# A down projection by seven products with the tokens moving, the last gate as modulation sections, the residual in device memory

## The chip, the cores and the metric

The kernel runs on one core of a Trainium2 chip. The metric is device time in microseconds (us) of one execution; the figure given for a kernel is the median of its runs. TensorE (PE) multiplies, VectorE (DVE), ScalarE (ACT) and GpSimd (POOL) work elementwise, and SyncE (SP) issues nearly all transfers between device memory and the on-chip memory.

## The reference

One layer of a diffusion backbone is applied to 128 context tokens and 512 latent tokens, all in float32, D_MODEL = 1024, D_FF = 2816. The context tokens are modulated by `c_ctx`, the latent ones by `c`; the weights are shared.

```python
mod = (silu(cond) @ w_ada + b_ada)[:, None, :]
sh1, sc1, g1, sh2, sc2, g2 = split(mod, 6, axis=-1)
h = rms(x, norm_mix) * (1 + sc1) + sh1
mix, k, v = mixer(h, ...)              # attention and a gated short convolution, output projection
x = x + g1 * mix
h2 = rms(x, norm_ffn) * (1 + sc2) + sh2
gate, up = split(h2 @ w_gate_up, 2, axis=-1)
x = x + g2 * ((silu(gate) * up) @ w_down)
```

The last gate `g2` is one section of the modulation: 1024 numbers for the context, 1024 for the latent tokens. The outputs are x of both kinds of tokens, and the context's k and v.

## The kernel before

All 640 tokens (`TOK`) are worked on together, as five tiles of 128 (`TORD`: the context first, then four latent tiles); `HALF` is 320 of them. Every float32 product is made as three products of rounded halves: `split` (lines 151 and 152) makes a high part on ScalarE and the rest on VectorE, and `mm3` (lines 155 to 157) multiplies high by high, high by low and low by high into one PSUM bank.

**The stages**, in us from the start of the span: until 50 the first modulation sections, normalisation and h; until 251 the projections of q, k, v, the attention, and between its steps the convolution and the modulation sections (2) to (4); until 314 the output projection with the residual `x2`, the second normalisation and the transposes into `h2` (`h2_turn`, line 1012); then the feed-forward until the end.

**Modulation sections** are made by `ada_all`: for each half section of 512 columns four loads (`aw`, 512 KB each, `AWB` = 2 buffers) and eight matmuls of a padded copy of the conditioning vectors (`cond_mm`, line 394) into one bank, then four small transposes that sum the bank's strips (line 446), then an evict that adds the bias. It is a generator: it is a part of the `filler`, and at every `F1` in the order `SEQ` one step of the filler is emitted between steps of the attention.

**The last gate** is made in another way. `g2_step` (lines 1032 to 1043) multiplies rows of w_ada by one conditioning number per partition and accumulates, on VectorE, 128 x 512 at a time; `g2_out` (lines 1045 to 1052) sums over the partitions by a matmul with ones (line 1051), which leaves the gate on all partitions, and adds the bias. The first half is done during the output projection, the second during the first down projection.

**The feed-forward** takes w_gate_up in 22 blocks of 128 rows, f = 0 to 21. The first two (`NPLAIN`) are plain products. Each of the others is one product of 2 x 2 blocks (gate and up by the two halves of D on the weights' side, the two halves of D by the two halves of the tokens on the other) made by seven products in place of eight (Winograd's form): `ff_a` to `ff_end`, lines 1214 to 1257. The weights' operands are the blocks A11, A12, A22, A21 and the sums S1 to S4, made by `op_load` (lines 194 to 217: sums on VectorE at line 206, then `split`); the activations' operands B and T are made once from `h2` (`b_plain`, `b_sums`). Each product is four k-steps of three matmuls of 128 x 320: the weights are stationary, the 320 tokens move. Where two sums share a partial sum, ScalarE copies the bank into a second one (line 1241 for instance) and TensorE adds to both.

**The down projection** comes after each of four groups of blocks (`GCUT` = 0, 6, 12, 17, 22), in `down` (lines 1256 to 1294). Here the split activations `gT` are stationary, 128 tokens each, and rows of w_down move, 512 columns (in the last group's last tile 256):

```python
mm3(ps[:, :n], gT[f][0][:, s], gT[f][1][:, s], wh[:, i, c0:c0 + n], wl[:, i, c0:c0 + n],
    f == grp[0], f == grp[-1])
```

For each of two column halves and five token tiles one bank is summed over the group, multiplied by the gate (line 1291, `dm`), and added to `x2` (line 1292). In the last group the sum is stored from there. So `x2`, the residual, stays on chip from the output projection to the end.

**What sets the order.** On TensorE the order is written out by hand all through. On the other engines it is by hand until the second plain block is done, and after that a scheduler places each instruction by priority (`early(n)` moves one forward). All loads are issued by SP in one planned order (`plan`, then `W` takes them), a fixed number ahead of their use, into rings: `wf` of three buffers for raw weights, `wh` and `wl` of four for operands. PSUM in the feed-forward is six banks for products ("f") and two for transposes.

Of the kernel before, what the change touches and what calls it, by code (L numbers as in the profile page):

```python
# [9 lines left out]
F32 = mybir.dt.float32  # L10
# [28 lines left out]
SEQ = ('c0 k1 q4 k4 C0 k0 K4 Q4 a0 q0 F1 k2 K0 a1 t0 k3 t1 K1 o0 F1 Q0 o1 K2 K3 q1 F1 S0.0 F1 F1 F1 S0.1 F1 '  # L39
# [10 lines left out]
GCUT = [0, 6, 12, 17, 22]  # L50
# [25 lines left out]
AWB = 2  # L76
# [7 lines left out]
PLACE = 48, 72  # L84
# [7 lines left out]
def build(ctx, tc, x_prompt, x_sample, c, cache_k, cache_v, c_ctx, norm_mix, norm_ffn, w_ada, b_ada,  # L92
# [76 lines left out]
    open_pool("F", "right", "placeF of y oz ysum m0 g1 rs5 cp")  # L169
# [24 lines left out]
    def op_load(e):  # L194
# [3 lines left out]
        a11, a12, a21, a22 = g[:, 0:4], g[:, 4:8], u[:, 0:4], u[:, 4:8]  # L198
        if name[0] == "S":
            if name == "S12":  # L200
                sums[f] = T("sx", (P, 8, P), F32, 2)
            s13, s24 = sums[f][:, 0:4], sums[f][:, 4:8]
            with early(SOP[f >= NPLAIN]):
                for out, x, y, op in {"S12": ((s13, a21, a22, ALU.add), (s24, s13, a11, ALU.subtract)),
                                      "S34": ((s13, a11, a21, ALU.subtract), (s24, a12, s24, ALU.subtract))}[name]:
                    dve.tensor_tensor(out, x, y, op)  # L206
            src = sums[f]
        else:
            src = {"A1": g, "A2": u, "A22": a22}[name]
        if name == "A22":  # L210
            w = T(("wh", "wl")[ops[0] % 2], (P, 2, 4, P), F32R, WHB)
            ops[0] += 1
            e[5] = w[:, 0], w[:, 1]
        else:
            e[5] = T("wh", (P, 8, P), F32R, WHB), T("wl", (P, 8, P), F32R, WHB)
        with early(SOP[f >= NPLAIN]):
# [54 lines left out]
    ADA = [(2, 0), (2, 1), (3, 0), (3, 1), (4, 0), (4, 1)]  # L271
# [6 lines left out]
    for n, (off, ct) in enumerate(CONV + [(None, 0)]):  # L278
        if off is not None:
            plan(("conv", off, ct), wi[:, :, off + ct * P:off + (ct + 1) * P])  # L280
        for sec, j, h in ada_steps[2 * n - 2:2 * n if off is not None else None] if n else ():
            col = sec * D + j * 512
            plan(("ada", sec, j, h), wa[:, 2 * h:2 * h + 2, col:col + 512], 1, "a")
    for j in range(2):
        for kp in range(4):
            plan(("o", j, kp), wo[:, 2 * kp:2 * kp + 2, j * 512:(j + 1) * 512], 2 * j, "w", V_AON + 2 * kp)
        for kp in range(0 if j else 4):
            plan(("ada", 5, j, kp), wa[:, 2 * kp:2 * kp + 2, 5 * D + j * 512:5 * D + (j + 1) * 512], 2, "f")

    GROUPS = [list(range(a, b)) for a, b in zip(GCUT, GCUT[1:])]  # L290
    PLAIN, PRODS = ("A1", "A2"), ("A1", "S12", "A22", "S34")
    PAIRS = {"A11": ("A1", 0), "A12": ("A1", 4), "A21": ("A2", 0), "A22": ("A2", 4),
             "S1": ("S12", 0), "S2": ("S12", 4), "S3": ("S34", 0), "S4": ("S34", 4)}

    def plan_raw(f, x, ph=3):
        col = f * P + (DFF if x == "u" else 0)
        plan((x, f), wg[:, :, col:col + P], ph, "f")
# [5 lines left out]
    G2KP = {0: (0,), 1: (1,), 2: (2, 3)}  # L303
    for gi, grp in enumerate(GROUPS):
        for f in grp:
            ph = 2 if f < NPLAIN else 3
            plan_raw(f, "g", ph)
            plan_raw(f, "u", ph)
            plan_ops(f, PLAIN if f < NPLAIN else PRODS, ph)
        for j in range(2):  # L310
            for i0 in range(0, len(grp), 2):
                n = len(grp[i0:i0 + 2])
                plan(("d", grp[i0], j), wd[:, grp[i0]:grp[i0] + n, j * 512:(j + 1) * 512], 2)
                if gi == 0 and j == 0:
                    for kp in G2KP[i0 // 2]:
                        plan(("ada", 5, 1, kp), wa[:, 2 * kp:2 * kp + 2, 5 * D + 512:6 * D], 2, "f")
# [414 lines left out]
    def conv_steps(ct):  # L731
# [22 lines left out]
        for i, _ in enumerate(conv_mm(O_GB, ct, bps)):  # L754
# [4 lines left out]
            yield  # L759
        ysq = ysum if ct == 0 else T("c25", (P, PADW), F32, 3)[:, :PADW - 2]  # L760
# [6 lines left out]
    def ada_all():  # L767
        for sec, j in ADA:
            rp = PB(tag="c")
            for h in range(4):  # L770
# [3 lines left out]
                if h == 1:  # L774
                    yield
# [11 lines left out]
            else:  # L787
                ps = mod_sum(res, 4, "c")
                if sec == 4:
                    mod_evict(1, 4 * j, 4, ps, None)  # L790
                else:
                    mod_evict(1, 4 * j, 4, None, ps)

    ada_gen = ada_all()
# [17 lines left out]
    filler = itertools.chain(*(conv_steps(ct) for ct in range(4)), ada_some(12))  # L812
    NFILL = 12 * 6 + 12
# [178 lines left out]
    open_pool("X", "left", "x2 x2n g2 sx")  # L992
    open_pool("GT", "left", "gT")
    open_pool("Y1", "left", "B11 B21")
    open_pool("D", "right", "mix mx aacc bb")
# [6 lines left out]
    x2n = {}  # L1002
    TORD = [CTX] + list(range(NL))
# [24 lines left out]

    g2 = [T("g2", (P, D), F32, 2) for _ in range(2)]
    g2acc = [None, None]  # L1030

    def g2_step(j, kp):

        w = W(("ada", 5, j, kp))
        for i in range(2):
            k = 2 * kp + i
            for cc in range(2):
              with early(G2P) if G2P and j == 0 else ExitStack():
                if k == 0:
                    g2acc[cc] = T("cg", (P, TOK), F32, 2)[:, :512] if j else T("aacc", (P, 512), F32, 2)  # L1040
                    dve.tensor_scalar_mul(g2acc[cc], w[:, i], cs[:, k, cc:cc + 1])
                else:
                    dve.scalar_tensor_tensor(g2acc[cc], w[:, i], cs[:, k, cc:cc + 1], g2acc[cc], ALU.mult, ALU.add)

    def g2_out(j):
        cols = slice(j * 512, (j + 1) * 512)
        bb = T("cu", (P, TOK), F32, 2)[:, :512] if j else T("bb", (P, 512))
        sp.dma_start(bb, b_ada[0, 5 * D + j * 512:5 * D + (j + 1) * 512].partition_broadcast(P))
        for cc in range(2):
            ps = PB()  # L1050
            pe.matmul(ps, ones, g2acc[cc], start=True, stop=True)
            dve.tensor_tensor(g2[cc][:, cols], ps, bb, ALU.add)


# [25 lines left out]
    def b_sums(part):  # L1080
# [4 lines left out]
        def diff(x, y, z):  # L1085
            w[x] = T("tr", (P, 4, 192), F32, 3)[:, :, :n]
# [11 lines left out]
    for j in range(2):  # L1098
        cols = slice(j * 512, (j + 1) * 512)
        for n, t in enumerate(TORD):  # L1100
# [26 lines left out]
            if j == 0 and G2N <= n < 4 + G2N:  # L1127
                g2_step(0, n - G2N)
            if j == 1 and n == 0:
                g2_out(0)  # L1130
# [251 lines left out]
```

## Time and profile before

| | us |
|---|---|
| median of 3 runs | 747.73 |
| lowest and highest of them | 747.54, 748.13 |
| the profiled execution's own time | 747.58 |
| its span | 745.8 |
| TensorE busy | 729.5 (98%) |
| VectorE busy | 529.8 (71%) |
| ScalarE busy | 375.6 (50%) |
| GpSimd busy | 48.6 (7%) |

The times of instructions come from one profiled execution, whose span starts with the first and ends with the last thing recorded; its own time is 1.8 us longer. TensorE's matmuls overlap in the record, since a product's start does not wait for the end of the one before it: what a product takes from the time is the distance between two starts, not its duration. The granted clock is full in all slices.

### The profile page before, as it was taken

How to read it: one execution, taken by the hardware profiler on the slowest of the kernel's cores; microseconds unless marked ns; L12 is line 12 of the kernel's file. 1: busy time of each engine (PE TensorE's matmuls, PEld its weight loads, DVE VectorE, ACT ScalarE, POOL GpSimd, SP SyncE). 2: the span in 40 equal slices, each digit the busy share in tenths (PEclk: the TensorE clock that was granted, in tenths of full speed). 3: DMA queues.
4: the chain of work that ended last, by engine and by line, in shares of the span. 5: the costliest groups of instructions: out<-in, count | busy, mean ns of one | idle time of the engine just before them, and what ended most of it. 6: DMA issues, size and time to landing. Idle time of an engine off the chain costs nothing.

```text
span 745.8 us, 11640 instructions
## 1 busy us (share of the span) xinstructions
PE 729.5 (98%) x4556; PEld 657.5 (88%) x4556; DVE 529.8 (71%) x905; ACT 375.6 (50%) x701; POOL 48.6 (7%) x85
## 2 busy tenths in 40 slices
PE   7999899999999999999999999999999999999997
PEld 5568878988998887899998799998899998899986
DVE  5668878685666797888869767864668765677653
ACT  5357877676766544765552135552135541354510
POOL 2403201002010210000000000000000000000000
PEclk9999999999999999999999999999999999999999
DMA  9985133523424363032336314224014132123312
GB/s 288 294 248 165 43 113 104 167 93 117 152 92 147 109 225 114 26 89 57 114 97 195 89 31 112 76 95 142 28 57 113 57 113 86 57 75 96 105 65 85
DMA packets 101387, 84.50 MB, mean 113 GB/s; under 512 B 3502, under 2 KB 81650, under 8 KB 101332
## 3 DMA queue, kind: packets, MB, share of 16 engines
q1 hardware_dynamic: 100980, 83.39, 36.6%
q8 instruction: 36, 0.59, 0.4%
q0 software_dynamic: 352, 0.37, 0.3%
q14 instruction: 19, 0.16, 0.1%
HBM read 79.68 MB, written 2.75 MB: 111 GB/s over the span
## 4 chain that ended last, share of the span: by engine, by line
PE 85%; DVE 6%; DMA 3%; ACT 3%; issue 2%; POOL 1%; SPq 0%; ACTq 0%; DVEq 0%; POOLq 0%
PE pf L155 19%; PE pf L156 19%; PE pf L157 19%; PE pc L723 3%; PE pc L725 3%; PE pc L724 3%; PE pt L862 3%; PE po L879 2%; PE ps L835 2%; PE pc L394 2%; PE ph L156 1%; PE ph L157 1%; PE ph L155 1%; DMA es<-t 1%; DMA af<-in_w_ada_dram 1%
## 5 line engine op out<-in xcount | busy, mean ns | idle before, releaser
L151 ACT ACTIVATE wh<-wf 128x1024 fp32r<-128x1024 f32 (+1 forms) x68 | 65.7, 969 | 107.3 <-PE pf L157 67.0
L152 DVE TENSOR_TENSOR wl<-wf,wh 128x1024 fp32r<-128x1024 f32 (+1 forms) x58 | 69.2, 1195 | 59.2 <-ACT wh L151 45.2
L155 PE MATMUL pf<-B,wh 128*128 128x320 f32 x288 | 89.1, 309 | 0.0
L157 PE MATMUL pf<-B,wl 128*128 128x320 f32 x288 | 89.1, 309 | 0.0
L156 PE MATMUL pf<-B,wh 128*128 128x320 f32 x288 | 89.0, 309 | 0.0
L155 PE MATMUL pf<-wh,gT 128*128 128x512 f32 (+1 forms) x225 | 86.9, 386 | 0.0
L155 PE MATMUL pf<-T,wh 128*128 128x320 f32 x280 | 86.7, 310 | 0.0
L156 PE MATMUL pf<-wl,gT 128*128 128x512 f32 (+1 forms) x225 | 86.5, 385 | 0.0
L156 PE MATMUL pf<-T,wh 128*128 128x320 f32 x280 | 86.5, 309 | 0.0
L157 PE MATMUL pf<-T,wl 128*128 128x320 f32 x280 | 86.5, 309 | 0.0
L157 PE MATMUL pf<-wh,gT 128*128 128x512 f32 (+1 forms) x225 | 86.5, 384 | 0.0
L151 ACT ACTIVATE wh<-sx 128x1024 fp32r<-128x1024 f32 x40 | 42.4, 1060 | 61.7 <-DVE sx L206 22.9
L152 DVE TENSOR_TENSOR wl<-sx,wh 128x1024 fp32r<-128x1024 f32 x40 | 49.0, 1225 | 28.5 <-ACT wh L151 24.9
L723 PE MATMUL pc<-hH,wh 128*128 128x320 f32 x192 | 61.0, 318 | 0.9 <-DVE modt L448 0.9
L725 PE MATMUL pc<-hH,wl 128*128 128x320 f32 x192 | 59.3, 309 | 0.0
L724 PE MATMUL pc<-hL,wh 128*128 128x320 f32 x192 | 59.3, 309 | 0.0
L157 PEld LDWEIGHTS pf<-B,wl 128*128 128x128 f32 x288 | 54.1, 188 | 0.1
L155 PEld LDWEIGHTS pf<-B,wh 128*128 128x128 f32 x288 | 54.1, 188 | 0.1
L156 PEld LDWEIGHTS pf<-B,wh 128*128 128x128 f32 x288 | 54.1, 188 | 0.1
L155 PEld LDWEIGHTS pf<-T,wh 128*128 128x128 f32 x280 | 52.5, 188 | 0.5 <-ACT pf L1241 0.3
L156 PEld LDWEIGHTS pf<-T,wh 128*128 128x128 f32 x280 | 52.6, 188 | 0.0
L157 PEld LDWEIGHTS pf<-T,wl 128*128 128x128 f32 x280 | 52.5, 188 | 0.0
(302 smaller groups left out, 1669.4 us busy)
## 6 DMA issues: line engine op xcount, KB each, us to landing
wf<-in_w_gate_up_dram SPq DMA_DIRECT2D x44, 512.0 KB, 4.1
aw<-in_w_ada_dram SPq DMA_DIRECT2D x24, 512.0 KB, 4.3
wf<-in_w_down_dram SPq DMA_DIRECT2D x20, 512.0 KB, 4.2
wf<-in_w_in_dram SPq DMA_DIRECT2D x18, 512.0 KB, 5.8
af<-in_w_ada_dram SPq DMA_DIRECT2D x32, 256.0 KB, 6.4
x<-in_x_sample_dram SPq DMA_DIRECT2D x8, 512.0 KB, 6.2
wf<-in_w_out_dram SPq DMA_DIRECT2D x8, 512.0 KB, 3.5
wf<-in_w_ada_dram SPq DMA_DIRECT2D x8, 512.0 KB, 3.9
```

Of the source, the lines that this page charges most:

```text
L151: act.activation(hi, src, AF.Copy)
L152: dve.tensor_tensor(lo, src, f32(hi), ALU.subtract)
L155: pe.matmul(out, lh, rh, start=start, stop=False, skip_group_check=more)
L156: pe.matmul(out, lh, rl, start=False, stop=False, skip_group_check=more)
L157: pe.matmul(out, ll, rh, start=False, stop=stop, skip_group_check=more)
L394: pe.matmul(out[CG * g:CG * (g + 1)], cp[:, k], w, start=(k < 4), stop=(k >= KD - 4), skip_group_check=True)
L723: pe.matmul(acc, wh[:, k], hH[k][:, c0:c0 + n], start=(k == 0), stop=False)
L724: pe.matmul(acc, wh[:, k], hL[k][:, c0:c0 + n], start=False, stop=False)
L725: pe.matmul(acc, wl[:, k], hH[k][:, c0:c0 + n], start=False, stop=(k == KD - 1))
L835: pe.matmul(s2[:, g, :320], q, kk[:, v, P + g * 320:P + (g + 1) * 320], start=(i == 0), stop=(i == 1))
L862: pe.transpose(tp[:, i, h], u[3][h][:, kt * P:(kt + 1) * P], ident)
L879: pe.matmul(ov, w, x[:, i].rearrange("p a q -> p (a q)"), start=(g == 0 and i == 0 and n == 0), stop=(last and i == len(kts) - 1 and n == 1))
```

## The change

**Down by seven products.** `down(gi, c)` is called for each group and for each of four blocks of 256 output columns. It uses the seven products of the feed-forward: the weights' side is a 2 x 2 block of w_down (two halves of 128 output columns by two halves of the group's rows), its operands made by the same `op_load`; the activations' side is the two halves of the group's rows by the two halves of the tokens, and its operands T1 to T4 are made pair by pair in `ff_out`. The weights are stationary and the 320 tokens move; the result stands with the output columns on partitions. The groups become 4, 6, 6 and 6 rows, so that all are even, and the two rows of a pair are taken from the two halves of the group. A product has half as many k-steps as the group has rows: two or three.

**Gathering and turning back.** `gather` adds the four quarters of a block into 16 accumulators of 128 x 320 that take the place of `x2`. In the last group `gate` multiplies the accumulators by the gate on ScalarE, the evict multiplies the new sum by the gate while it adds, and `finish` turns each block back with ten transposes (40 in all), adds the residual and stores it: 20 stores of 128 x 256.

**Last gate.** Section 5 is added to `ada_all`, in the form that has output columns on partitions (`g2T`); `g2_step`, `g2_out` and their bias loads are gone. A half section's eight matmuls are emitted in one step, with a step's pause after its evict; `SEQ` is written anew; `AWB` becomes 4.

**Residual.** After the second normalisation `x2` is stored to a tensor in device memory, `xd`, by five stores on SP's queue, and in the last group, after its first block, five loads bring it back (`x_back`).

Smaller: the slices of `b_sums` are 160 and 160 in place of 192 and 128, ScalarE copies u2 into a half of `cg`, and pools are arranged anew.

```diff
-GCUT = [0, 6, 12, 17, 22]
+GCUT = [0, 4, 10, 16, 22]
-AWB = 2
+AWB = 4
...
+    xd = [T("xd", (P, D), F32, NT) for _ in range(NT)]
...
+                    sp.dma_start(xd[n], x2[t])
...
+                if sec == 5:
+                    dve.tensor_tensor(g2T[:, 4 * j:4 * j + 4, :], ps,
+                                      vec[:, 40 + 4 * j:44 + 4 * j].unsqueeze(2).to_broadcast([P, 4, 2]), ALU.add)
...
     def ff_out(f, cu):
+        k, odd = divmod(f - group_of(f)[0], 2)
         with early(GSP):
-            split(gT[f][0], gT[f][1], cu)
+            if not odd:
+                w = T("gT", (P, 2, 4, HALF), F32R, GB)
+                t1 = T("tr", (P, 2, HALF), F32, 3)[:, 0]
+                split(w[:, 0, 0], w[:, 1, 0], cu[:, LO])
+                dve.tensor_tensor(t1, cu[:, HI], cu[:, LO], ALU.subtract)
+                split(w[:, 0, 1], w[:, 1, 1], t1)
...
+            dve.tensor_tensor(t23[:, 0], cu[:, HI], t1, ALU.subtract)
+            c2 = cu.rearrange("p (a n) -> p a n", a=2)
+            split(w[:, 0, 2:4], w[:, 1, 2:4], c2)
+            dve.tensor_tensor(t23[:, 1], cu[:, HI], cu0[:, HI], ALU.subtract)
+            t4 = T("tr", (P, 2, HALF), F32, 3)[:, 0]
+            dve.tensor_tensor(t4, cu[:, LO], t23[:, 0], ALU.subtract)
+            split(v[:, 0, 0:2], v[:, 1, 0:2], t23)
+            split(v[:, 0, 2], v[:, 1, 2], t4)
...
+    def gather(gi, x, part, ps, add=None):
+        w = acc_of(x, part)
+        if gi == len(GROUPS) - 1:
+            y = ys[x][:, part]
+            for cut, cc in ((slice(0, P), 1), (slice(P, HALF), 0)) if part is LO else ((slice(0, HALF), 0),):
+                g = g2T[:, x, cc:cc + 1]
+                if add is not None:
+                    dve.scalar_tensor_tensor(w[:, cut], add[:, cut], g, w[:, cut], ALU.mult, ALU.add)
+                dve.scalar_tensor_tensor(y[:, cut], ps[:, cut], g, w[:, cut], ALU.mult, ALU.add)
+        elif gi:
+            if add is not None:
+                dve.tensor_tensor(w, add, w, ALU.add)
+            dve.tensor_tensor(w, ps[:, :HALF], w, ALU.add)
+        elif add is None:
+            act.activation(w, ps[:, :HALF], AF.Copy)
+        else:
+            dve.tensor_tensor(w, ps[:, :HALF], add, ALU.add)
...
+    TURNS = (3, 4), (0, 1), (2,)
+    def finish(c, ns):
+        cols = slice(2 * c * P, (2 * c + 2) * P)
+        tp = PB((P, len(ns), 2, P))
+        for i, n in enumerate(ns):
+            for h in range(2):
+                pe.transpose(tp[:, i, h], ys[2 * c + h][:, n * P:(n + 1) * P], ident)
+        out = xr[ns][:, :, cols]
+        with early(CPP):
+            dve.tensor_tensor(out, tp.rearrange("p n a q -> p n (a q)"), out, ALU.add)
+        for i, n in enumerate(ns):
+            sp.dma_start(o_dram[TORD[n]][:, cols], out[:, i])
...
+    def down(gi, c):
...
+        prod(b1, d, "A11", "B11")
+        copy(b2[:, :HALF], b1)
+        prod(b3, d, "S1", "T1")
+        copy(keep[:, LO], b3)
+        turn()
...
+        p(b1, "S2", "T2", some)
...
+        copy(keep[:, HI], b1)
+        if last:
+            gate(x)
+            gate(y)
+        p(b2, "A12", "B21", rest or some)
+        gather(gi, x, LO, b2)
+        turn()
+        p(b3, "S4", "B22", first)
+        p(b1, "S3", "T3", range(n))
+        copy(b4[:, :HALF], b1)
+        gather(gi, y, HI, b1, keep[:, LO])
+        p(b3, "S4", "B22", range(len(first), n))
+        turn()
+        p(b4, "A22", "T4", range(n))
+        gather(gi, x, HI, b3, keep[:, HI])
+        gather(gi, y, LO, b4)
```

More of the change, by code (lines that the diff above doesn't have):

```diff
@@ L759, in conv_steps @@
             yield
+            if i == 2:
+                yield from ada_some(1)
         ysq = ysum if ct == 0 else T("c25", (P, PADW), F32, 3)[:, :PADW - 2]
@@ L792, in ada_all @@
                     mod_evict(1, 4 * j, 4, None, ps)
+            yield
+    g2T = T("g2T", (P, KD, 2))
     ada_gen = ada_all()
@@ L810, in conv_rms @@
             rB[t] = r[:, t:t + 1]
-    filler = itertools.chain(*(conv_steps(ct) for ct in range(4)), ada_some(12))
-    NFILL = 12 * 6 + 12
+    filler = itertools.chain(*(conv_steps(ct) for ct in range(4)), ada_some(16))
+    NFILL = 12 * 6 + 16
     used = [0]
@@ L1027, in build @@
     mixed, ms0 = {}, {}
[L1029 to L1052, printed above, removed]
     B = {}
@@ new lines, in down, with turn, copy, p @@
+    def down(gi, c):
+        d, n, last = (gi, c), len(GROUPS[gi]) // 2, gi == len(GROUPS) - 1
+        x, y = 2 * c, 2 * c + 1
+        todo = [lambda i=i: finish(c - 1, i) for i in TURNS] if last and c else []
+        def turn():
+            if todo:
+                todo.pop(0)()
+        def copy(out, src):
+            with early(CPP):
+                act.activation(out, src[:, :HALF], AF.Copy)
+        b1, b2 = FB(), FB()
+        prod(b1, d, "A11", "B11")
+        copy(b2[:, :HALF], b1)
+        b3 = FB()
+        prod(b3, d, "S1", "T1")
+        keep = T("cg", (P, TOK), F32, 2)
+        copy(keep[:, LO], b3)
+        turn()
+        cut = n - 1 if c == 0 else n
+        some, rest = range(cut), range(cut, n)
+        def p(out, a, b, ks):
+            if ks:
+                prod(out, d, a, b, start=False, more=True, ks=ks)
+        p(b1, "S2", "T2", some)
+        if rest:
+            p(b2, "A12", "B21", some)
+            p(b1, "S2", "T2", rest)
+        copy(keep[:, HI], b1)
[5 more added lines that the diff above has]
+        turn()
+        first = range(1) if rest else range(0)
+        p(b3, "S4", "B22", first)
+        p(b1, "S3", "T3", range(n))
+        b4 = FB()
+        copy(b4[:, :HALF], b1)
[5 more added lines that the diff above has]
+        gather(gi, y, LO, b4)
@@ L1326, in build @@
                     ff_end(f)
-        down(gi, grp)
-        for f in grp:
-            del gT[f]
+        last = gi == len(GROUPS) - 1
+        for cb in range(NC):
+            down(gi, cb)
+            if last and cb == 0:
+                x_back()
+    for ns in TURNS:
+        finish(NC - 1, ns)
     pe_order.__exit__(None, None, None)
-    for n in ("psum", "G", "Y2", "Y1", "GT", "X", "A"):
+    for n in ("psum", "G", "Y3", "Y2", "Y1", "GT", "X", "R", "A"):
         close_pool(n)
```

197 lines of the change are left out of this document (97 added, 100 removed), and 20 rows, old and new, of the table SEQ.

## The prediction

> **What bounds the kernel now.** I read the page first: busy time, slices, chain.
>
> ```profile
> span 745.8 us, 11640 instructions
> PE 729.5 (98%) x4556; PEld 657.5 (88%) x4556; DVE 529.8 (71%) x905; ACT 375.6 (50%) x701; POOL 48.6 (7%) x85
> PE   7999899999999999999999999999999999999997
> PE 85%; DVE 6%; DMA 3%; ACT 3%; issue 2%; POOL 1%; SPq 0%; ACTq 0%; DVEq 0%; POOLq 0%
> ```
>
> TensorE works 98% of the span and stands idle only in the first and the last slice. The view of waits agrees (engine and line, who it waited for, us in total, times, longest): these two lead it, all below are shorter.
>
> ```profile
> PE pt L382 <- ACT crow L380: 3.0, 1, 3.0
> PE ps L155 <- ACT hH L486: 1.0, 1, 1.0
> ```
>
> The windows over the FFN say it again: a stretch of gate/up blocks (433 to 507) and one with a down projection (605 to 639) are full, at full clock, while VectorE is at 71 and 58%, ScalarE at 54 and 28%.
>
> ```profile
> core 0: us, PE busy (x) PEld busy (x) DVE busy (x) ACT busy (x) POOL busy (x), PEclk, DMA share, GB/s
> 433.00:507.00 74.00, 74.00 (x500) 73.57 (x499) 52.34 (x72) 39.95 (x65) 0.00 (x0) 1.00 0.29 86
> 605.00:639.00 34.00, 34.00 (x168) 29.34 (x167) 19.72 (x27) 9.67 (x13) 0.00 (x0) 1.00 0.28 86
> ```
>
> So an instruction taken from TensorE is time, unless another engine comes to set the pace. Busy time overstates a product (durations overlap), so its price is the pitch between starts. From the timeline, first and last of three runs: 48 products of 320 columns in 7.04 us, 33 of 512 in 7.49, 17 of 256 in 2.03.
>
> ```profile
> 700.10 0.31 PE L156 MATMUL pf<-T,wh 128*128 128x320 f32 x1
> 707.14 0.31 PE L156 MATMUL pf<-T,wl 128*128 128x320 f32 x1
> 708.13 0.40 PE L155 MATMUL pf<-wh,gT 128*128 128x512 f32 x1
> 715.62 0.39 PE L155 MATMUL pf<-wh,gT 128*128 128x512 f32 x1
> 739.52 0.28 PE L155 MATMUL pf<-wh,gT 128*128 128x256 f32 x1
> 741.55 0.28 PE L157 MATMUL pf<-wh,gT 128*128 128x256 f32 x1
> ```
>
> That is 0.1467, 0.227 and 0.119 us: a slope of 1/2.4 ns a column and some 13 ns a product.
>
> **Part 1, the down projection's products.** Each mm3 is one product on each of lines 155 to 157, so the rows of line 155 are a third.
>
> ```profile
> L155 PE MATMUL pf<-wh,gT 128*128 128x512 f32 x215 | 84.1, 391 | 0.0
> L155 PE MATMUL pf<-wh,gT 128*128 128x256 f32 x10 | 2.8, 282 | 0.0
> ```
>
> Before: 645 x 0.227 + 30 x 0.119 = 150.0 us. After, eleven pairs of rows x 4 column blocks x 7 products x 3 = 924 of 320 columns, the shape of gate/up: 924 x 0.1467 = 135.5. **Minus 14.5.** Multiplications fall by an eighth, the fixed 13 ns is paid 249 times more.
>
> The Trainium skill has a rule against this ("TensorE: Matmul & The Clock Gate", Back-to-back issue gap): a stream of weight loads and products is said to sustain 131 ns at 512 columns and 81 at 128. Interpolated, an estimate, 320 would be 106 and 256 some 98, and the down projection would go from 87 to 98 us, 10 slower. The trace has 227 and 147; the same section's isolated gap, N/2.4 + 2.5, would give minus 16.9.
>
> **Part 2, the last gate.** Its partial products go from VectorE into TensorE's modulation sections.
>
> ```profile
> 182.09 0.44 PE pc L446 x4
> 182.53 0.99 PE pc L394 x8
> 286.71 1.72 PE pt L1051 x4
> 319.55 0.87 PE pt L1012 x8
> 413.51 1.72 PE pt L1051 x4
> ```
>
> Off the stream: twice the matmul by ones, 2 x 1.72, **minus 3.4**. Onto it: two sections of 16 records (8 took 0.99) and four transposes (0.44): 4 x 0.99 + 2 x 0.44 = 4.8, taken as **plus 4.5**, since sixteen now stand in one stretch (bounds 4.1 to 4.9). Eight 512 KB loads move into the attention. AWB goes from 2 to 4, so a section's four loads can be there when its stretch starts; landing takes
>
> ```profile
> aw<-in_w_ada_dram SPq DMA_DIRECT2D x24, 512.0 KB, 4.3
> L394 PE MATMUL pc<-aw,cp x96: 592/605/617, 94.0 to 249.7; 128*32 128x512 f32 x96
> ```
>
> 4.3 us each, 17 for four, and eight stretches in these 156 us stand about 20 apart: the lead hides them. Cover gone, a stretch waits for one landing, 4.3.
>
> VectorE loses the 32 multiply-accumulates of some 0.75 us, some in the output projection, where its chain is late once:
>
> ```profile
> PE ph L156 <- DVE wl L252: 0.4, 1, 0.4
> ```
>
> **Minus 0.5** (0 to minus 1.3, three such waits). The residual's five stores go into SP's queue among the first gate/up loads; an issue costs 0.45, five 2.3:
>
> ```profile
> 260.75 1.35 SPq L1133 DMA_DIRECT2D x<-in_x_sample_dram  x3
> wf<-in_w_gate_up_dram SPq DMA_DIRECT2D x44, 512.0 KB, 4.1
> ```
>
> Behind a waiting store stand loads that the queue planned three ahead; nothing waits until 2.3 + 4.1 exceed that lead. I take zero; the price with the cover gone is 2.3.
>
> **Part 3, turning back.** Forty transposes; thirty stand in the last group's stream at 0.87 for eight: **plus 3.5** (3.3 to 3.7; their evictions fall to VectorE). The last ten are the tail.
>
> ```profile
> 742.33 0.42 DVE L1292 TENSOR_TENSOR x<-dm,x 128x256 f32<-128x256 f32 x1
> out_dram<-x SPq DMA_DIRECT2D x2, 128.0 KB, 1.7
> ```
>
> Today the span ends 4.25 us after the last product starts (741.55) and 3.05 after the last VectorE add ends. After: product 0.3, two multiply-adds of 128 and 192 columns (0.75), four transposes 0.44 and a hand-over, an add of 512 wide (0.69), the rest of the adds and two transposes (0.4), then the same 3.05, with up to 0.45 for the queue of five issues: 5.8 to 6.3. **Plus 1.9** (1.6 to 2.1). Residual reloads have three column blocks, some 18 us, of cover.
>
> The groups become 4, 6, 6 and 6 rows; pool sizes, slices of 160 and the tile u2 that becomes a half of cg move no instruction in number or width that counts: zero.
>
> **Part 4, VectorE and ScalarE.** Down's weights were split once and evicted with multiply and add; now every block has operand sums, three-way splits and six evictions. Rows:
>
> ```profile
> L152 DVE TENSOR_TENSOR wl<-sx,wh 128x1024 fp32r<-128x1024 f32 x40 | 49.0, 1225 | 28.5 <-ACT wh L151 24.9 <-PE pf L157 3.6
> L206 DVE TENSOR_TENSOR sx<-wf 128x512 f32<-128x512 f32 x20 | 13.8, 692 | 10.1 <-DMA wf<-in_w_gate_up_dram 9.9
> L1243 DVE TENSOR_TENSOR cu<-pf,p 128x320 f32<-128x320 f32 x20 | 9.7, 485 | 1.9 <-ACT pf L1241 1.9
> L152 DVE TENSOR_TENSOR gT<-cu,gT 128x640 fp32r<-128x640 f32 x22 | 18.1, 821 | 4.8 <-ACT gT L151 4.8
> ```
>
> On a line through these, 384 wide is 0.55 and 768 is 0.955. A six-row group then asks of VectorE, for each row: sums 4 x 0.69, splits 3 x 1.225 + 0.69, evictions 4 x 0.485, activation operands 2.5, together 11.6; for each column block 4 x 0.55 + 3 x 0.955 + 0.55 + 6 x 0.485 = 8.5. So 6 x 11.6 + 4 x 8.5 = 103.6 us, against TensorE's 756 products x 0.1467 = 110.9. Independent neighbours overlap by 0.085 (625.11 + 0.69 ends behind the next start):
>
> ```profile
> 625.11 0.69 DVE L206 TENSOR_TENSOR sx<-wf 128x512 f32<-128x512 f32 x1 [0.77 <-DMA wf<-in_w_gate_up_dram]
> 625.72 0.69 DVE L1291 TENSOR_TENSOR dm<-pf,g 128x512 f32<-128x512 f32 x1
> 626.32 0.68 DVE L206 TENSOR_TENSOR sx<-sx,wf 128x512 f32<-128x512 f32 x1
> ```
>
> so the 155 operations need between 90 (all overlapped) and 108 (a gap of 0.03 before each). VectorE goes from 71 to between 81 and 97%. I take the middle: it keeps up, with little slack. ScalarE, by the same count, asks 66 to 75 of 110.9.
>
> The Trainium skill's "VectorE: DVE Perf Modes" (The TRN2 errata) asks for tiles of 512 elements or more, as each instruction pays a fixed latency; the block's are 320 and 384 wide. Its formula for the add gives, an estimate, 0.491 us at 320; the trace has 0.485, so the sum stays.
>
> Hand-overs: in a block, ScalarE copies a bank three times before TensorE adds to the copy.
>
> ```profile
> 703.77 0.31 PE L157 MATMUL pf<-T,wl 128*128 128x320 f32 x1
> 704.11 0.42 ACT L1241 ACTIVATE pf<-pf 128x320 f32<-128x320 f32 x1 [0.95 <-PE pf L157]
> ```
>
> The copy ends 704.53, 0.61 after its product's slot, 0.67 with the release. TensorE has meanwhile at least one k-step set, 0.44 (group of four rows) or 0.88 to 1.32 (six): short by 0.2 in the first group's few places, covered later, unless ScalarE is busy. Of the start of f = 2, the row
>
> ```profile
> 347.56 1.23 DVE L152 TENSOR_TENSOR wl<-sx,wh 128x1024 fp32r<-128x1024 f32 x1 [0.72 <-ACT wh L151]
> 350.17 0.31 PE L155 MATMUL pf<-T,wh 128*128 128x320 f32 x1
> ```
>
> ends (348.79) 1.4 us before the products of S34, the second row, in a stretch where VectorE has no gap from 338 and now gets 2 to 4 us of activation operands more: 0.5 or so late. **Plus 1** for all these (0 to 3).
>
> **Sum.** Against the profiled run's own 747.58 us (span 745.8; the median of the runs is 747.73): -14.5 - 3.4 + 4.5 - 0.5 + 3.5 + 1.9 + 1.0 = -7.5, **740.1 us**. All bounds the good way: -10.2, 737.4; the bad way -4.2, 743.4. Its own range is 737 to 744. What measurement can tell from no change is 0.2%, 1.5 us.
>
> **Rivals.** Late operands. The sums of today wait 10.1 us in 20 for a load, and a block's loads are wanted every 9.2 us (63 x 0.1467) from a ring of three. If each of sixteen blocks comes 0.25 to 0.3 us late: +4.4, 744.5. For: those waits; against: they have not reached TensorE so far. 0.14.
>
> Attention. The hand-made order is new, and a stretch of sixteen wants four loads at once: one landing lost, 4.3, 744.5. Against: 20 us apart. 0.04.
>
> VectorE sets the pace: slower. Where an operand is ScalarE's high half and then VectorE's low half, VectorE waits today 24.9 us in 40 splits, 0.6 each. A six-row group has 55 such pairs; if each keeps a third of that, 0.22, the 103.6 become 115.7, which is 4.8 over TensorE's 110.9; three groups, 14.4, less the 1.0 of stalls already counted: 753. It decides once a group asks more than 110.9 + 2.5 (three of those eat the 7.5). For: 108 at the gaps alone, and an order fixed by the scheduler, so a late operand holds up the evictions queued behind it; against: 90 with all overlap, and an engine with slack fills such waits with other work. 0.11.
>
> A product's fixed cost. If weight loads showed under the products, f ns each instead of 13, the first term would be -17.6 us (645 x 512 + 30 x 256 - 924 x 320 columns at 1/2.4 ns) + 249 f, and the whole nothing at f = 43; at 60 it is -2.7 and the time 752. Against: gate/up shows 13 in the same shape. 0.03. (The Trainium skill's sustained figures in "TensorE: Matmul & The Clock Gate", Back-to-back issue gap, point this way; the trace does not.)
>
> That the change doesn't do as it says would take the first term away; the built program has the 924 products of 320 columns and none of 512 on pf, so no chance is kept for it.
>
> **How the numbers follow.** 740.1 has 0.68. Of late operands' 0.14, 0.10 are faster and 0.04 within 0.2%; of the attention's 0.04, half and half. Faster 0.68 + 0.10 + 0.02 = 0.80, same 0.06, slower 0.11 + 0.03 = 0.14. The range goes from 736.5 (the good bounds and a us for the new order in the attention) to 747, which takes in both 744.5 cases with their spread; the slower ones are left out.
>
> **What would show it.** Right: 2796 products of 320 columns at a pitch of 0.147; no 128x512 on pf; the FFN's slices still 9; VectorE at 81 to 97% in a six-row group; last product to end about 6 us. Wrong: windows of groups two to four longer than 111 us with VectorE full and TensorE's waits naming wl or sx (VectorE), or wf (loads); pitch above 0.147; waits in 94 to 250 on aw; the wait for ScalarE's copy more than 0.3 each.

## The result, and the profile after

The changed kernel takes 754.19 us (median, 752.9 to 754.53) against 747.8 us of the kernel before: ratio 1.0072, interval 1.006 to 1.0085. Forecast were 740.1 us, with a range to 747. In a second group of runs it took 752.71 us beside 747.95 (ratio 1.0065, 1.0049 to 1.0082). So it is slower by 5 to 6 us where 7.5 were to be saved, and the question is where some 13 us went.

The page of the changed kernel, the same lines as before:

```profile
span 751.1 us, 12704 instructions
PE 728.3 (97%) x4877; PEld 676.5 (90%) x4877; DVE 578.0 (77%) x1072; ACT 443.5 (59%) x872; POOL 49.4 (7%) x85
PE   7999899999999999999999999999999999999997
PE 76%; DVE 9%; ACT 6%; DMA 5%; issue 3%; POOL 0%; SPq 0%; ACTq 0%; DVEq 0%; POOLq 0%
```

Tenths hide it: the slices of the feed-forward are still 9, yet TensorE's share of the chain fell from 85 to 76%, and ScalarE and transfers rose on it from 3% each to 6 and 5%. The view of waits over the feed-forward names them (before, it has no line for this stage):

```profile
PE pf L155 <- ACT cg L1345: 3.3, 6, 1.4
PE pf L155 <- ACT cg L1248: 2.5, 4, 0.7
PE pf L156 <- DVE gU L152: 0.7, 1, 0.7
```

Lines 1248 and 1345 are ScalarE's copies of a bank before TensorE adds to that bank again. The view counts 6.5 us; the distances between starts show more, because a product's place is lost and the first product after a wait takes 0.25 us instead of 0.147:

```profile
457.74 0.31 PE L157 MATMUL pf<-B,wl 128*128 128x320 f32 x1
458.68 0.41 PE L155 MATMUL pf<-T,wh 128*128 128x320 f32 x1 [0.64 <-ACT cg L1248]
458.93 0.31 PE L156 MATMUL pf<-T,wh 128*128 128x320 f32 x1
```

From 457.74 to 458.93 stand 1.19 us for two products that take 0.29 elsewhere. So I counted products off in the trace (84 for a row, 42 or 63 for a block of a group of four or six) and compared the time of each stretch with its products at 0.1467. What is over, in us, here and in the experiments told below (in the last group's blocks the thirty transposes add 3.8 everywhere, and they hold no other loss; they are left out):

| kernel | rows of groups 1 to 4 | blocks of groups 1 to 3 | sum |
|---|---|---|---|
| changed | 1.0, 1.6, 1.0, 0.8 | 3.6, 2.5, 1.4 | 11.9 |
| long runs | 1.0, 0.2, 0, 0 | 4.0, 1.2, 1.1 | 7.5 |
| ring of four | 1.0, 0, 0, 0 | 2.9, 1.1, 1.1 | 6.1 |
| copies first | 0.6, 0.6, 0.8, 2.1 | 2.8, 2.3, 1.3 | 10.5 |
| less vector work | 0.4, 0.4, 0.1, 0.1 | 2.8, 2.1, 1.4 | 7.2 |

How well such a sum is known, three more profiles of the same feed-forward show: 12.2 in a second profile of the changed kernel, 10.4 in the experiment with the old attention, 13.1 in that with the residual from the input. So the 10.5 of "copies first" is inside the spread, and the other three rows are well below it.

**How a stall arises** is best seen at the largest, at the end of the second group. The chain of waits of the changed kernel's second profile, TensorE's pieces left out:

```profile
503.42 4.75 DMA wf<-in_w_gate_up_dram
508.17 0.02 issue
508.19 0.70 DVE sx L211
508.89 0.02 issue
508.92 0.70 DVE sx L211
509.62 0.02 issue
509.64 0.04 ACTq L151
509.68 0.05 issue
509.72 0.07 ACT wh L151
509.79 0.89 issue
510.69 0.43 ACT cg L1345
```

A load lands after 4.75 us; VectorE has waited for it and makes two sums; ScalarE takes the high half of them (0.97 us until the next can start); only then, though its bank was ready, comes the copy that stands next in ScalarE's order, and TensorE waits for that copy. Every engine works in its order here, so the lateness of a load is handed through three of them. In the first profile the same place costs 1.36 us, and there the load is not the last thing that ScalarE waits for:

```profile
509.55 0.69 DVE L211 TENSOR_TENSOR sx<-sx,wf 128x512 f32<-128x512 f32 x1
510.36 1.06 ACT L151 ACTIVATE wh<-sx 128x1024 fp32r<-128x1024 f32 x1 [2.10 <-PE pf L156]
```

The sums end at 510.24; the product of line 156 that the high half waits for ends at 510.29, and holds it up presumably because it still reads the buffer that the high half is to take (the view names the product, not the buffer). So the ring of four operands may stand close behind the loads in this chain; a longer one was not tried. In the first profile VectorE's waits over the feed-forward were

```profile
DVE sx L211 <- DMA wf<-in_w_gate_up_dram: 16.1, 18, 2.2
DVE sx L211 <- DMA wf<-in_w_down_dram: 8.6, 12, 1.4
```

24.7 us, against 9.9 in the kernel before.

### The profile page after: what moved, and what is told of

It is laid out like the page before. It is cut to its first block, busy times and chain, and to the rows that moved or that the text cites. A ratio compares the mean times of both kernels' runs of the same rounds, so it can differ in the third digit from the quotient of the medians.

```text
span 751.1 us, 12704 instructions
## 1 busy us (share of the span) xinstructions
PE 728.3 (97%) x4877; PEld 676.5 (90%) x4877; DVE 578.0 (77%) x1072; ACT 443.5 (59%) x872; POOL 49.4 (7%) x85
## 4 chain that ended last, share of the span: by engine, by line
PE 76%; DVE 9%; ACT 6%; DMA 5%; issue 3%; POOL 0%; SPq 0%; ACTq 0%; DVEq 0%; POOLq 0%
PE pf L155 15%; PE pf L156 15%; PE pf L157 15%; PE pc L736 3%; PE pc L737 3%; PE pc L738 3%; PE pc L407 3%; PE ph L155 2%; PE ph L157 2%; PE ph L156 2%; PE pt L880 2%; PE ps L853 2%; DMA wf<-in_w_gate_up_dram 2%; DMA es<-t 2%; PE po L897 2%
## 5 line engine op out<-in xcount | busy, mean ns | idle before, releaser
L151 ACT ACTIVATE wh<-sx 128x1024 fp32r<-128x1024 f32 (+2 forms) x72 | 67.7, 940 | 66.2 <-DVE sx L211 42.4
L152 DVE TENSOR_TENSOR wl<-sx,wh 128x1024 fp32r<-128x1024 f32 (+2 forms) x72 | 77.4, 1075 | 19.8 <-ACT wh L151 13.7
L151 ACT ACTIVATE wh<-wf 128x1024 fp32r<-128x1024 f32 (+4 forms) x68 | 58.5, 863 | 21.9 <-PE pf L156 13.2
L152 DVE TENSOR_TENSOR wl<-wf,wh 128x1024 fp32r<-128x1024 f32 (+2 forms) x50 | 55.7, 1115 | 17.5 <-ACT wh L151 12.3
L156 PE MATMUL pf<-gT,wh 128*128 128x320 f32 x192 | 59.4, 310 | 0.0
L157 PE MATMUL pf<-gT,wl 128*128 128x320 f32 x192 | 59.3, 309 | 0.0
L155 PE MATMUL pf<-gT,wh 128*128 128x320 f32 x192 | 59.3, 309 | 0.0
## 6 DMA issues: line engine op xcount, KB each, us to landing
af<-in_w_ada_dram SPq DMA_DIRECT2D x32, 256.0 KB, 6.0
```

The lines of the kernel that those rows point to most:

```text
L151: act.activation(hi, src, AF.Copy)
L152: dve.tensor_tensor(lo, src, f32(hi), ALU.subtract)
L155: pe.matmul(out, lh, rh, start=start, stop=False, skip_group_check=more)
L156: pe.matmul(out, lh, rl, start=False, stop=False, skip_group_check=more)
L157: pe.matmul(out, ll, rh, start=False, stop=stop, skip_group_check=more)
```

## The experiments

Three theories stood at first: **L**, loads come too late to their ring of three, and what is queued behind the waiting instruction is late with them; **V**, VectorE's work sets the pace; **C**, ScalarE's order puts operand copies ahead of bank copies.

**Long runs.** In the raw loads of rows 2 to 21 and of w_down, each partition's bytes come in one piece:

```diff
-                plan((x, f), wg[:, :, col:col + P], ph, "f")
+                plan((x, f), wg[:, :, col:col + P] if f < NPLAIN else wg[:, f % KD, off:off + D].rearrange("p (a b) -> p a b", b=P), ph, "f")
...
-                plan((x, d), wd[:, grp[0]:grp[0] + len(grp), (2 * cb + i) * P:(2 * cb + i + 1) * P], 3, "f")
+                plan((x, d), wd[:, grp[0] + (2 * cb + i) % len(grp), :len(grp) * P].rearrange("p (a b) -> p a b", b=P), 3, "f")
```

> The raw weights of the down projection and of gate/up rows 2 to 21 are read from other places of the same tensors, so that each partition's bytes stand in one piece of 2 to 4 KB instead of pieces of 512 bytes (the numbers computed are others; bytes, buffers and the order on every engine stay as they are). Theory L (loads come too late to a ring of three; an engine waiting for one holds up the copies queued behind it): landing falls from 4.3 to 4.8 us to about 3, VectorE's waits for wf fall from 24.7 us to under 12, and the time falls by 5 to 10 us to 744 to 749. Theory V (VectorE's own work sets the pace) and theory C (ScalarE's order puts operand copies ahead of the bank copies that TensorE waits for): 754.2 within 1.5.

747.83 us (ratio to the kernel before 0.9999, 0.999 to 1.0008): 5 to 6 us less, with the same order on every engine but SP. The rows of the transfers, of the changed kernel and then of this one, and VectorE's waits of this one:

```profile
wf<-in_w_gate_up_dram SPq DMA_DIRECT2D x44, 512.0 KB, 4.8
wf<-in_w_down_dram SPq DMA_DIRECT2D x24, 384.0 KB, 4.3
```

```profile
wf<-in_w_gate_up_dram SPq DMA_DIRECT2D x44, 512.0 KB, 3.8
wf<-in_w_down_dram SPq DMA_DIRECT2D x24, 384.0 KB, 3.6
DVE sx L211 <- DMA wf<-in_w_gate_up_dram: 6.8, 9, 2.1
DVE sx L211 <- DMA wf<-in_w_down_dram: 4.5, 5, 1.5
```

Landing fell less than expected (3.8 and 3.6, not 3), the waits as expected (11.3), and the stalls by 4.4. Nothing but the source of the loads was touched, so L holds for that part; V and C had expected 754.2.

**Ring of four.** Room for a fourth raw buffer (`wu`) comes from the ring of operand sums:

```diff
-        wf = T("aw", (P, a, b), F32, AWB) if ring == "a" else T("wf", (P, a, b), F32, WFB)
+        wf = T("aw", (P, a, b), F32, AWB) if ring == "a" else T("wu", (P, a, b)) if ring == "f" and key[1] in SUMMED and next(nraw) % 4 == 0 else T("wf", (P, a, b), F32, WFB)
...
-                sums[f] = T("sx", (P, 8, P), F32, 2)[:, :2 * n]
+                sums[f] = T("sx", (P, 8, P), F32, 1)[:, :2 * n]
```

> A fourth buffer for raw weights in the feed-forward; the room comes from the operand sums' ring, one buffer instead of two. Theory L: loads are issued half a row earlier, the 13 us of stalls in the feed-forward fall to 5 or less, 745 to 748, unless the single buffer for sums gives some of it back. V and C: 754.2 within 1.5.

746.0 us, ratio 0.9976 (0.9965 to 0.9987): it beats the kernel before and the changed one, and is in L's range, though the stalls, 6.1, stay above the 5 that L allowed. VectorE waits for no load in this stage any more. The windows of the third group (its rows, its blocks, both), the changed kernel's first:

```profile
515.86:590.81 74.95, 74.22 (x507) 73.93 (x505) 60.19 (x95) 41.28 (x73) 0.00 (x0) 1.00 0.31 86
590.81:629.15 38.34, 37.70 (x254) 36.95 (x253) 34.04 (x62) 26.86 (x55) 0.00 (x0) 1.00 0.29 82
515.86:629.15 113.29, 111.91 (x758) 110.88 (x757) 94.23 (x156) 68.14 (x128) 0.00 (x0) 1.00 0.30 84
```

```profile
510.61:584.53 73.92, 73.92 (x506) 73.92 (x505) 59.98 (x95) 41.43 (x73) 0.00 (x0) 1.00 0.32 86
584.53:622.59 38.06, 37.72 (x254) 36.97 (x253) 34.20 (x62) 26.88 (x55) 0.00 (x0) 1.00 0.31 84
510.61:622.59 111.98, 111.64 (x758) 110.89 (x757) 94.18 (x156) 68.31 (x128) 0.00 (x0) 1.00 0.31 85
```

The rows take 73.92 us, which is 504 times 7.04/48, the pitch without waits, with the same 94 us of VectorE's work. V, as the pace of a group, is refuted: with 94 of 112 us of work VectorE does not hold TensorE up. What stays is 1.1 us in each block stage of six rows, and 2.9 in the group of four.

**Copies first.**

```diff
-            with early(CPP):
+            with early(400):
                 act.activation(out, src[:, :HALF], AF.Copy)
```

(and so at the other four copies.)

> The scheduler's priority of ScalarE's bank copies in the feed-forward goes from 50 to 400; three to eight copies move ahead of an operand's high half on ScalarE. Theory C: TensorE's waits for the copies (lines 1248 and 1345: 5.8 us in ten, and their restarts) fall to under 3, time 748 to 751. L: the copies come sooner where they moved, the loads as late as before, 752 to 755. V: 754.2 within 1.5.

750.34 us (ratio 1.0037, 1.0022 to 1.0053). The time is in C's range and below L's, but C is not borne out as a cause of its own: the two waits stayed at 5.4 us, where C expected under 3, and the stalls fell by 1.4 only, which is inside their spread, of the 2.4 to 3.9 between the medians.

```profile
PE pf L155 <- ACT cg L1345: 3.0, 6, 1.3
PE pf L155 <- ACT cg L1248: 2.4, 2, 1.8
```

**Less vector work.** In `ff_out`, for the odd row of a pair:

```diff
-            dve.tensor_tensor(t23[:, 0], cu[:, HI], t1, ALU.subtract)
...
-            split(v[:, 0, 0:2], v[:, 1, 0:2], t23)
-            split(v[:, 0, 2], v[:, 1, 2], t4)
+            for i, x in enumerate(("T2", "T3", "T4")):
+                dops[x, k] = w[:, 0, i + 1], w[:, 1, i + 1]
```

> The activations' operands T2, T3 and T4 of the down projection are not made; T1, B21 and B22 stand in their place. VectorE loses 2.8 us and ScalarE 1.8 us for each pair of rows, 31 and 20 us in all; loads, sums and copies stay. Theory V: stalls vanish, 742 to 746. L: stalls of the blocks stay, since sums wait for loads and not for work; 750 to 754. C: the waits in the last rows of a group, where these copies stand ahead, go; 750 to 752.

747.62 us (0.9998, 0.9988 to 1.0007), outside all three ranges. L expected 750 to 754: VectorE still waits nearly as much for loads,

```profile
DVE sx L211 <- DMA wf<-in_w_gate_up_dram: 14.5, 14, 2.2
DVE sx L211 <- DMA wf<-in_w_down_dram: 8.0, 13, 1.3
```

and yet the stalls fell from 11.9 to 7.2, where V expected none. Taken with the ring, this means that a late load alone doesn't stop TensorE, nor does the work alone; VectorE and ScalarE, with less to do, catch up after a late load before TensorE wants their results. (The loads of w_gate_up also landed in 4.2 us here, against 4.8 and 4.5 in the two profiles of the changed kernel, so a part may be theirs.) The two are factors of one loss, not two losses: either taken away saves 4.7 to 5.8.

**The old attention.** `SEQ`, the plan of loads and `ada_all` as before, and a copy of the bias in the gate's place:

```diff
-    ADA = [(2, 0), (2, 1), (3, 0), (3, 1), (4, 0), (4, 1), (5, 0), (5, 1)]
+    ADA = [(2, 0), (2, 1), (3, 0), (3, 1), (4, 0), (4, 1)]
...
+    dve.tensor_copy(g2T, vec[:, 40:48].unsqueeze(2).to_broadcast([P, KD, 2]))
```

> The last gate's two sections, their loads and the new order in the attention are taken back (the attention is that of the kernel before; the gate is left at its bias). Theory G (the sections cost what their matmuls, transposes and new waits take in the attention, 6.7 us of the trace): 747 to 748.5, the output projection starting at 251 as before. Prediction's own price, 4.5: 749.7. If the feed-forward's stalls hang on when it starts or on loads that come later, the feed-forward changes from 426.8 by more than 2.

745.7 us (0.9969, 0.9959 to 0.9978), against 752.71 of the changed kernel in the same group: 7.0 less. That is under theory G's 747 to 748.5, which was reckoned from 754.2; as a difference it fits G's 6.7. The first product of the output projection, of this kernel and then of the changed one in its first profile:

```profile
251.61 0.39 PE L155 MATMUL ph<-wh,m 128*128 128x512 f32 x1
```

```profile
257.69 0.48 PE L155 MATMUL ph<-wh,m 128*128 128x512 f32 x1
```

In the changed kernel's profile of this group it starts at 256.93, so 5.3 of the 6.2 us between the two spans are in the attention. The feed-forward, 425.8 us here, hardly depends on it (427.0 in the changed kernel of this group).

**The residual from the input.**

```diff
-                    sp.dma_start(xd[n], x2[t])
...
-                sp.dma_start(xr[ns][:, h], xd[n])
+                sp.dma_start(xr[ns][:, h], x_dram[TORD[n]])
```

> The five stores of the residual are left out and what is loaded back in the last group is the input x, so 2.6 MB less are written. Theory: the stores cost nothing, the first rows of the feed-forward stand as before, 754.2 within 1. Rival: the stores stand in SP's queue in front of the first gate/up loads and make the first group late (its rows and blocks are 4.6 over their products): 750 to 752.

752.16 us beside 752.71 (both under the 754.2 within 1 that was expected); the first group's rows and blocks stand at 25.65 and 28.28 us, in the changed kernel at 25.65 and 28.01. The stores cost nothing that can be measured; the rival is out. The other run of that group was the changed kernel itself:

> The changed kernel once more, beside the runs of this group. All theories: 754.2 within 1; if it comes out lower, the differences of the first four experiments shrink by as much.

752.71 us, as told above: 1.5 us under the first group's median and outside the range, so differences to the changed kernel are known to a microsecond or two, and those of the first four experiments may be 1.5 us smaller.

**Ring and copies** is the ring's edit and the copies' together.

> The ring of four of the second experiment and the priority of copies of the third together. If a late load and a copy behind an operand copy are two links of one chain (L), the ring takes nearly all and the copies add 0 to 1.5: 744.5 to 746. If they are separate causes (L and C), the gains add: 742 to 743.5.

746.51 us (0.9979, 0.9969 to 0.999), 0.5 above L's range and far from the other. The attention took longer here (its end is at 258.6 us, with the ring alone at 256.2), so the feed-forward decides: 420.6 us against 420.9 with the ring alone. The copies add nothing that can be measured once the loads are in time, which fits one chain and not two causes.

**The small group last**: the ring of four and

```diff
-GCUT = [0, 4, 10, 16, 22]
+GCUT = [0, 6, 12, 18, 22]
```

> The ring of four, and the groups 6, 6, 6 and 4 rows in place of 4, 6, 6 and 6. In the second experiment the group of four rows still loses 2.9 us in its blocks, the groups of six 1.1 each, the last one (where transposes stand in the hand-overs) nothing. Theory H (what is left is ScalarE's copy of a bank, about 0.67 us, against a cover of 0.44 in blocks of two k-steps): the first group loses about 1.1 like other groups of six, the last group's transposes cover its short blocks, 1.5 to 2 us less than the second experiment's 746.0, 744 to 744.5. Rival B (the first group loses because it is first, with VectorE full after the plain rows): the loss stays in the first group whatever its size, 745.5 to 746.5.

748.44 us (0.9998, 0.9989 to 1.0008), above both ranges. Half of theory H came out: the first group, now of six rows, loses 1.1 us in its blocks as the others do, so the 2.9 belonged to blocks of two k-steps and not to being first. The other half failed: the last group's blocks took 32.0 us where products (24.6) and transposes (3.8) make 28.4, and the wait is a new one, in three places, for VectorE's last gated sum before a block is turned back:

```profile
PE pt L1326 <- DVE B L1291: 2.4, 3, 1.0
```

**The gate as cover.** The old attention, the ring of four, and section 5 in `down`, a fourth of a half section for each block of groups one and two:

```diff
+            w = W(("g2", gi, c))
+            for i in range(2):
+                cond_mm(gate_sum[gi], 2 * c + i, w[:, i])
```

> The attention of the kernel before, the ring of four, and the last gate's two sections made in the feed-forward: one step of two rows of matmuls (0.46 us of TensorE) in each of the eight blocks of the first two groups, between the product before a bank copy and the product that waits for it. Theory H: part of the added 4.4 us of TensorE work stands in stalls of 4 us that it takes away; with the fifth experiment's 745.7 for the old attention, less 5 for the ring, the time is 742 to 743.5. If added work covers nothing, 745 to 745.5. If its eight loads make operands late again, over 746.

750.97 us (1.0034, 1.0023 to 1.0045): a miss, mainly by the price of a step. TensorE's timeline at one of them, and the chain at one stretch of the changed kernel:

```profile
372.07 1.05 PE L409 MATMUL pt<-wf,cp 128*32 128x512 f32 x4
373.05 0.41 PE L155 MATMUL pf<-gT,wh 128*128 128x320 f32 x1
```

```profile
121.03 1.85 PE pc L407 x16
```

Four records take 0.98 us (372.07 to 373.05), sixteen in one stretch 1.85: strips of 32 columns run side by side, and a fourth of a half section fills only two of the four strips. The product before a step and the first one behind it take 0.24 and 0.25 us to the next start, 0.1 more than others, so a step costs 1.18 us and eight cost 9.4, not 3.7; the feed-forward grew by 9.8 against the ring alone.

The cover itself worked where blocks have three k-steps. In the second group's blocks TensorE's time is that of products, steps and four transposes, and the 1.1 us that stood there with the ring alone are gone. In the third group's, four transposes of the gate's second half stand where TensorE waited for ScalarE, and the blocks take 38.04 us, not more than the 38.06 without them:

```profile
595.00 0.60 PE L461 MATMUL pt<-ident,tr 128*128 128x128 f32 x4
589.72:627.76 38.04, 37.98 (x258) 37.39 (x257) 34.37 (x64) 26.86 (x55) 0.00 (x0) 1.00 0.30 84
```

In the first group's blocks, of two k-steps, the stalls stayed (3.4 beside the steps, 2.9 with the ring alone). VectorE waits for loads again, 14.2 us in seven waits; 6.6 of these are in the second group's blocks, where TensorE lost nothing by them, and how far the others matter is not shown. A cover no dearer than the stall was not tried.

**Both together**, the steps of the ninth and the groups of the eighth:

> The two before together: gate steps in the blocks of the first two groups, groups of 6, 6, 6 and 4 rows. Theory H: the cover is long in groups of six already, so the gate's steps take away 1 us there and the last group's short blocks are covered by transposes: 741.5 to 743.5. Rival B: as the ninth, within 1.

750.88 us (1.0037, 1.0023 to 1.005), within 0.1 of the ninth, as rival B has it. The time alone says nothing of H, since the steps' price hides it, but the blocks do: the first group's, of three k-steps now, take 41.65 us against 38.03 in the eighth, 3.6 more for four steps of 1.18, so the 1.1 of stalls went as H expected. The last group's short blocks were not covered (32.3 us, as in the eighth).

## Why the prediction was wrong, step by step

In the profiled executions, from start to start of the stages:

| term | forecast | measured |
|---|---|---|
| products of the down projection | -14.5 | -14.5 |
| section 5 in the attention | +4.5 | +6.7 |
| output projection (ones, stalls) | -2.2 | -2.8 |
| ones in the first down projection | -1.7 | -1.7 |
| thirty transposes | +3.5 | +3.8 |
| new stalls in the feed-forward | +1.0 | +11.9 |
| end | +1.9 | +2.4 |

Less the 0.5 of small stalls that the feed-forward had before, this is the 5.3 us between the spans.

**Right.** The first term: 2796 products of 320 columns stand in the trace, and where nothing waits they go at 0.1467 (the third group's rows with the ring). The fixed cost of a product didn't grow; the sustained figures of the Trainium skill's "TensorE: Matmul & The Clock Gate" (Back-to-back issue gap), weighed there, are not borne out. The residual at zero (sixth experiment). VectorE's demand, 90 to 108 forecast for a group of six rows: 94.2 measured. ScalarE's, 66 to 75: 68.1 in the third group, and 62.9, a little under, in the second. Nearly right are the transposes and the end, 6.6 after the last product starts against 5.8 to 6.3: VectorE's last add ends 4.0 before the span does instead of 3.05, behind this row of SP's queue:

```profile
744.23 4.23 SPq L1331 DMA_DIRECT2D out_dram<-T  x6
```

**The step that failed** is "Plus 1 for all these (0 to 3)" in part 4. It priced the hand-overs and one late operand, each alone, with the engines' sums as a check that they keep up; and they do keep up. But a sum over 111 us says nothing of when each result is there. Late operands were set aside as a rival (0.14, plus 4.4) with the reason "they have not reached TensorE so far". Before, this was true. A likely reason, argued from the windows and not tested, is that down projections with less work for VectorE stood between the groups of rows, and that VectorE had a third of its time free to catch up. The change took both: blocks want two loads every 6 to 9 us from the same ring, and VectorE goes from 71 to 83% busy (94.2 of 113.3). With the ring of four 5.8 of the 11.9 are gone: those hang on the late loads. The other 6.1 are hand-overs and the first rows, which the part had at 1: in blocks of three k-steps 1.1 for a group instead of nearly nothing, in blocks of two 2.9 instead of "0.2 in the first group's few places", since a copy waits not only 0.67 for its product and itself but also for what stands before it on ScalarE; and 1.0 in the row of f = 2, forecast 0.5 for a late operand of VectorE, where the runs show a wait for ScalarE's copy at line 1248 (0.7). Of the prediction's own signs the one on copies showed it: the waits for ScalarE's copies were 5.8 us in ten, 0.6 each, where more than 0.3 was to mean wrong.

**The second miss** is the attention: 6.7 instead of 4.5 (5.0 to 7.6 in the nine profiles of the last section). The matmuls themselves were cheaper than I took them: eight stretches of 1.85 in place of twelve of 1.0 are +2.9, the twelve more transposes +0.8 (four of them stood in the output projection before), 3.7 in all. Waits make only 0.5 of the remaining 3: TensorE's lines in the view of waits, from 50 us to the output projection, add up to 4.9 us before and 5.4 now. Another 1.9 stand at the 160 products of 256 columns into `po`, 20.7 us from start to start before and 22.6 now, of which 0.5 is a wait. The rival that I had at 0.04 was another one, a lost landing; no wait for `aw` shows. The waits that grew (before: 0.9 and 0.3 us for the first two, none for the third):

```profile
PE ps L853 <- ACT pr L863: 1.5, 3, 0.7
PE ps L853 <- DVE KB L683: 0.8, 1, 0.8
PE po L897 <- DVE pl L152: 0.5, 1, 0.5
```

Which of the moved steps makes the 3 us was not tried apart, and their cause stays open; the fifth experiment shows only that they go when the old order comes back and the two sections go.

**The rivals.** The slower one, VectorE as pace, had the right sign and almost the time (753), by a mechanism that the ring refutes, so that its time came near by chance. It had VectorE waiting for ScalarE's high halves; these waits, of the changed kernel and then with the ring, grew while TensorE's stalls fell:

```profile
DVE wl L152 <- ACT wh L151: 25.6, 47, 2.7
DVE wl L152 <- ACT wh L151: 35.5, 50, 3.1
```

The sum of two small rivals with the hand-overs made the result, and each alone was priced as leaving the kernel faster; that they might come together wasn't in the chances.

## What to carry to other kernels

Where one engine is 98% busy and work is moved from it to the others, their total is not the test: look for what each operand waits for last, and whether the buffers of the raw data are freed early enough for the next load to land, as the engine that waits holds up everything in its queue. Here one more buffer for raw weights was worth 5.9 us of the feed-forward (426.8 to 420.9), 6.7 to 8.2 between the medians, and made the change a small gain (746.0 against 747.7 us), with nothing else touched but the room it took. Price a hand-over with what stands ahead of it on the copying engine, not with the copy alone.

## What the runs showed of the hardware

A matmul with a stationary of 128 x 32 shares TensorE with neighbours in other strips of columns: four records in 0.98 us, eight in 1.0 (the kernel before), sixteen in 1.85. The Trainium skill's "TensorEngine Tiling (Array Packing)" (Key Properties) says that such tiles operate in parallel. The trace agrees: at 372.07 two records of different strips start within 0.01 us, the next two 0.45 later. Two strips cost as much as four, so a set of strips that is cut into smaller steps gets dearer.

The first product after a wait of TensorE takes 0.25 us to the next start instead of 0.147, so each wait costs 0.1 more than the view of waits counts, and a product behind transposes 0.23 (739.37 to 739.60 in the eighth experiment).

With the same order on TensorE the attention ended between 256.0 and 258.6 us in nine profiles of kernels that do not differ before that point in TensorE's order (256.2 in the first experiment, 258.6 in the seventh). Of these 2.6 us, 1.5 are there before the convolution's first product (line 736), which starts between 71.8 and 73.3 us. That is a part of the changed kernel's spread of 752.1 to 754.6 us; its cause is open.
